# Second part of a hybrid diffusion layer: gates ahead of spatial mixing, small steps between gates, two-input work from POOL to DVE, attention output in buffers of its own

## The chip, the cores and the metric

The kernel runs on one core of one Trainium2 chip. The metric is the device time of one execution in microseconds (us), the median of three runs.

## What is computed

One layer over 2048 latent tokens of width 1024, in float32. Two token mixers read the same normalised and modulated input `h`; a sigmoid gate per channel merges them; an output projection and a layer norm close the first half, and a mixture of experts with a second layer norm the second half. The reference, cut:

```python
mod = silu(c) @ w_ada + b_ada
sh1, sc1, g1, sh2, sc2, g2 = split(mod, 6)
h = layernorm(x) * (1 + sc1) + sh1
q, k, v, u, vg, ga, gb = split_proj(h @ w_in)      # 512, 128, 128, 512, 512, 1024, 1024
y_attn = latent_attention(rope(q), rope(k), v, k_ctx, v_ctx, sink, mask)   # (2048, 512)
vn = layernorm(gelu(vg), gm_ln_g, gm_ln_b)         # in chunks of 128 tokens, 8 groups of 64
y_gm = gelu(u) * (gm_ws @ vn + gm_bs)              # spatial mixing: (128 x 128) per group
y = sigmoid(ga) * (y_attn @ w_pa) + sigmoid(gb) * (y_gm @ w_pb)
x = layernorm(ALPHA * x + g1 * (y @ w_o), ln1_g, ln1_b)
h2 = layernorm(x) * (1 + sc2) + sh2
x = layernorm(ALPHA * x + g2 * hier_moe(h2), ln2_g, ln2_b)   # router: 4 groups of 8 experts, top 1, top 2
```

## The kernel before

Every float32 product is made of three passes: an operand is split into a rounded high part (a copy on ACT) and a low part (a subtraction, usually on DVE), and high x high, low x high and high x low are added up in PSUM. `split` (L90) records both instructions, `wsplit` (L728) loads a weight piece of 128 x 1024 into one of `RAW` = 3 raw buffers and splits it into one of `WB` = 3 pairs `Wh`, `Wl`; `mm3` (L735) issues the three matmuls.

There are three parts. `pass1` does the modulation, the projections for attention and the attention itself. `pass2`, which the change is about, takes the tokens in four groups of 512. `moe` and `final` follow.

For each group g, `pass2` has these stages:

- `head(g)` (L782) multiplies `h` by the weights of u into four PSUM banks. It is also where u goes through Gelu (`gelu_u`, L806), where vg is loaded, put through Gelu, normalised (`ln_affine`, L774) and split, and where the spatial mixing (L820 to L827) stands. `MMB` = 4 banks exist for products, so the first gate can have a bank only when Gelu has emptied one.
- `gates(g, f)` (L852) makes both gates of the 128 output channels f: two products of 24 matmuls each and a sigmoid on ACT.
- `mixers(g)` (L830) transposes the spatial result on PE and splits it into `gh`, `gl`; it also loads the attention output, through the raw buffers of the weights, and splits it into `oh`, `ol`.
- `merge(f, ...)` (L864) multiplies both mixers by their weights (24 matmuls), applies the gates on DVE, adds the two halves on POOL (L872) and splits the sum into `yh`, `yl`.
- `out_proj` (L875) does the output projection for groups 0 to 2, with the low parts of its weights on POOL, and multiplies by g1. Group 3 goes through `last_tiles` (L1026) instead, whose instructions are put in order by a small planner with written durations; `wo_piece` (L928) has multiplied the weights by g1 on POOL before.

Between the steps f of a group, small work of other stages is inserted: in group 0 `rows_ada` (L747) makes the rows g1, sh2, sc2; in groups 1 to 3 the four tiles of the group before go through `norms` (L890: residual, layer norm, second norm, whose last multiply and add, L903 and L904, are on POOL), `logits` (L908) and `route_tile` (L1264, the router). `ln_stats` (L94) computes mean and variance on DVE and then, with three small POOL instructions, 1/sqrt(var + eps) and the shift.

The program is written in Python order, and the framework's scheduler decides the order on each engine: it takes ready instructions by a timing model, earlier written ones first, unless one is pinned with `keep_in_program_order`. Each engine then executes its own list strictly in that order. All loads of these stages are issued from SP's queue.

Of the kernel before, what the change touches and what calls it, by code (L numbers as in the profile page):

```python
# [18 lines left out]
P = 128  # L19
# [74 lines left out]
def ln_stats(k, pool, x, width, eps=None, pin=False):  # L94
# [606 lines left out]
def pass2(k):  # L701
    nc, tc, T = k.nc, k.tc, k.T
    k.late = k.ctx.enter_context(tc.tile_pool(name="late", bufs=1, reuse_waits="tile"))
    with ExitStack() as ctx:
# [42 lines left out]
        def rows_ada(dst, cb, one):  # L747
# [34 lines left out]
        def head(g):  # L782
# [19 lines left out]
            gm = []  # L802
            for n in ("gmg", "gmb"):
                gm.append(wk.tile([P, 512], F32, name="sg", tag="sg", bufs=2 * AHEAD + 2))
                nc.sync.dma_start(gm[-1], bcast_row(T[n], 512))
            def gelu_u(i):  # L806
                nc.scalar.activation(uy[:, 0, i, :], acc[i], AF.Gelu_apprx_tanh)  # L807

            for i in range(4):
                if i >= 2:  # L810
                    gelu_u(2 * i - 4)
                    gelu_u(2 * i - 3)
                vg = wk.tile([P, 512], F32, name="vg", tag="vg", bufs=2)
                nc.sync.dma_start(vg, k.vg_d[4 * g + i])
                nc.scalar.activation(vg, vg, AF.Gelu_apprx_tanh)
                ln_affine(vg, 512, gm[0], gm[1], vg)
                split(k, vv[:, 0, i, :], vv[:, 1, i, :], vg)
# [12 lines left out]
        def mixers(g):  # L830

            uy = st[g][1]
            gT, oT = [], []
            for j in range(4):
                tp = tr_bank()
                for i in range(4):
# [976 lines left out]
```

## Time and profile before

| | us |
|---|---|
| median of 3 runs (2435.75 to 2441.88) | 2441.51 |
| the profiled execution, its own time | 2448.21 |
| its span, first to last instruction | 2446.4 |
| busy PE | 2232.2 |
| busy DVE | 1749.7 |
| busy ACT | 1200.7 |
| busy POOL | 913.7 |

The profiled execution is 6.7 us above the median. PE is TensorE's matmuls, DVE is VectorE, ACT is ScalarE, POOL is GpSimd, SP is the engine whose queue issues the loads. Busy time is an average over stages with different limits. `pass2` lasts from about 556 us (the last attention matmul) to about 1500 us; the out projections of groups 0 to 2 end at about 794, 1024 and 1255 us.

### The profile page before, as it was taken

What the parts mean: (1) busy time and instruction counts of PE and PEld (TensorE: products, weight loads), DVE (VectorE), ACT (ScalarE), POOL (GpSimd) and SP (SyncE); (2) the same over time, 40 slices, a digit from 0 to 9 for tenths busy, and PEclk for the clock granted to TensorE, in tenths of its full rate; (3) what the DMA queues carried; (4) which work ended last, traced back from release to release, by engine and by line L of the source; (5) the groups of instructions that cost most, each with busy time, mean ns of one, the idle gap of its engine ahead of it and who ended that gap; (6) DMA issues with size and microseconds to landing.
All of it is one profiled execution on the core that took longest, in us unless ns stands there. A gap on an engine that the chain in (4) does not pass through costs nothing. (4 is left out here: it accounts for less than half of the span.)

```text
span 2446.4 us, 32062 instructions
## 1 busy us (share of the span) xinstructions
PE 2232.2 (91%) x11269; PEld 1827.5 (75%) x11269; DVE 1749.7 (72%) x2925; ACT 1200.7 (49%) x1655; POOL 913.7 (37%) x767
## 2 busy tenths in 40 slices
PE   7899999998999899989999998799999998999960
PEld 3799999986768787877877776577777786777750
DVE  3778888886763677468547877478897868758868
ACT  3566666665222433343333323266575756546645
POOL 2333333421003432344324354233452536225328
PEclk9999999999999999999999998799999999999995
DMA  8211111116564445444344434589998989868956
GB/s 300 67 53 57 57 56 40 48 40 225 184 213 136 158 138 160 151 147 146 104 138 155 137 88 189 185 281 319 327 340 271 330 253 326 267 196 321 344 161 250
DMA packets 126711, 449.88 MB, mean 184 GB/s; under 512 B 20762, under 2 KB 42194, under 8 KB 101972
## 3 DMA queue, kind: packets, MB, share of 16 engines
q1 hardware_dynamic: 113684, 405.82, 47.5%
q0 software_dynamic: 12864, 41.98, 7.6%
q8 instruction: 90, 1.47, 0.2%
q14 instruction: 73, 0.60, 0.1%
HBM read 383.18 MB, written 64.57 MB: 183 GB/s over the span
## 5 line engine op out<-in xcount | busy, mean ns | idle before, releaser
L91 DVE TENSOR_TENSOR mWl<-mraw,mWh 128x2048 fp32r<-128x2048 f32 x192 | 437.5, 2311 | 57.5 <-ACT mWh L91 56.6
L91 ACT CAST mWh<-mraw 128x2048 fp32r<-128x2048 f32 x192 | 359.0, 1906 | 104.3 <-PE h L1551 79.3
L1551 PE MATMUL h<-mWh,xh 128*128 128x512 f32 x784 | 219.3, 400 | 5.7 <-ACT xh L91 4.5
L738 PE MATMUL mm<-hh,Wl 128*128 128x512 f32 x512 | 207.1, 404 | 10.7 <-DVE Wl L91 10.5
L737 PE MATMUL mm<-hh,Wh 128*128 128x512 f32 x512 | 207.2, 405 | 8.9 <-ACT yh L807 8.3
L1598 POOL DMA_INDIRECT acc_d<-yo,lst x49 | 140.7, 2871 | 199.0 <-DVE yo L1592 131.4
L91 ACT CAST Wh<-raw 128x1024 fp32r<-128x1024 f32 x140 | 145.8, 1046 | 138.8 <-PE mm L739 56.0
L1551 PE MATMUL h<-mWl,xh 128*128 128x512 f32 x784 | 212.8, 393 | 0.0
L739 PE MATMUL mm<-hl,Wh 128*128 128x512 f32 x512 | 206.2, 403 | 0.0
L91 DVE TENSOR_TENSOR Wl<-raw,Wh 128x1024 fp32r<-128x1024 f32 x116 | 157.5, 1362 | 53.4 <-ACT Wh L91 53.2
L1551 PEld LDWEIGHTS h<-mWh,xh 128*128 128x128 f32 x784 | 145.3, 190 | 37.3 <-ACT xh L91 5.4
L1551 PEld LDWEIGHTS h<-mWl,xh 128*128 128x128 f32 x784 | 148.8, 190 | 32.0
L1597 POOL TENSOR_TENSOR yo<-yo,g2b 64x1024 f32<-64x1024 f32 x20 | 119.9, 5997 | 125.7 <-DVE yo L1595 117.9
L379 PE MATMUL pj<-wh,hTl 128*128 128x512 f32 (+1 forms) x400 | 147.5, 369 | 3.3 <-POOL hTl L361 2.6
L379 PE MATMUL pj<-wh,hTh 128*128 128x512 f32 (+1 forms) x400 | 148.5, 372 | 1.5 <-DVE hTh L360 1.4
L379 PE MATMUL pj<-wl,hTh 128*128 128x512 f32 (+1 forms) x400 | 148.2, 371 | 0.0
L1516 POOL DMA_INDIRECT xg<-h_d,lst x49 | 73.5, 1500 | 169.2 <-PE tr L1530 90.2
L1551 PE MATMUL h<-mWh,xl 128*128 128x512 f32 x464 | 127.6, 396 | 8.6 <-DVE xl L91 8.4
L872 POOL TENSOR_TENSOR sg<-sg 128x512 f32<-128x512 f32 x32 | 44.4, 1388 | 239.1 <-DVE sg L871 215.8
L537 DVE CUSTOM_DVE_ANT_0 Sb<-S,mask,sink 128x640 f32<-128x640 f32 (+1 forms) x128 | 110.2, 861 | 23.4 <-PE S L533 16.6
L738 PEld LDWEIGHTS mm<-hh,Wl 128*128 128x128 f32 x512 | 99.7, 195 | 35.7 <-DVE Wl L91 15.3
L1551 PE MATMUL y<-mWh,gh 128*128 128x512 f32 x392 | 112.6, 407 | 13.0 <-DVE gh L91 11.7
(387 smaller groups left out, 5688.3 us busy)
## 6 DMA issues: line engine op xcount, KB each, us to landing
mraw<-mw SPq DMA_DIRECT2D x192, 1024.0 KB
raw<-wf SPq DMA_DIRECT2D x96, 512.0 KB
raw<-ada SPq DMA_DIRECT2D x32, 512.0 KB
raw<-wo SPq DMA_DIRECT2D x32, 512.0 KB
x<-x SPq DMA_DIRECT2D x30, 512.0 KB
x<-ada SPq DMA_DIRECT2D x16, 512.0 KB
hT_d<-hf SPq DMA_DIRECT2D x32, 256.0 KB
raw<-hT_d SPq DMA_DIRECT2D x16, 512.0 KB
```

What stands on the lines that cost most here:

```text
L91: return k.nc.scalar.copy(hi, src), (eng or k.nc.vector).tensor_sub(lo, src, hi)
L379: ins = nc.tensor.matmul(box[0][:, :n], x[:, kc, ts], y[:, kc, c0:c0 + n], start=q == 0, stop=q == 3 * KC - 1)
L537: nc.vector.tensor_tensor_reduce(x[:, :nk], S[:, :nk], mask[:, mi, :nk], 1.0, sink[:, h:h + 1], OP.add, OP.max, mx[:, s:s + 1])
L737: nc.tensor.matmul(out, lh, rh, start=first, stop=False)
L738: nc.tensor.matmul(out, ll, rh, start=False, stop=False)
L739: nc.tensor.matmul(out, lh, rl, start=False, stop=last)
L872: nc.gpsimd.tensor_add(sg[0], sg[0], sg[1])
L1516: ins = nc.gpsimd.indirect_dma_start(out=xg[i][0:n, :], out_offset=None, in_=k.h2_d[:, :], in_offset=bass.IndirectOffsetOnAxis(ap=lists[s] ...
L1551: nc.tensor.matmul(accs[m], a[:, ks], b[:, c0:c0 + 512], start=first and i + j == 0, stop=last and j == 1 and i == len(t) - 1)
L1597: nc.gpsimd.tensor_tensor(yo[0:64], yo[0:64], g2[0:64], op=OP.mult)
L1598: nc.gpsimd.indirect_dma_start(out=k.acc_d[:, :], out_offset=bass.IndirectOffsetOnAxis(ap=l[0:n, j, 0:1], axis=0), in_=yo[0:n, :], in_offs ...
```

## The change

All of it is in `ln_stats` and in `pass2`.

- Order: `head` only issues the products. `gelu_u`, `norm_v` (one tile of vg), `spatial`, `gate` (one gate), `mixers` (spatial result only) and `attended` (attention output only) are functions of their own. The new order is: head, Gelu of u, vg tiles 0 and 1, both gates of f = 0, vg tiles 2 and 3, spatial mixing, then per f: first gate of f + 1, (at f = 0 the mixers), the small steps `between`, second gate of f + 1, merge of f, the steps `behind`.
- Small steps: in `between` the transposes and splits of the router's input (`logit_rows`) and the norms; in `behind` the router's matmuls, the first part of `route_tile` for tile t - 1 and its rest for tile t - 2. `rows_ada` moves to `between`, and its two matmuls are put off by one step (`finish`).
- From POOL to DVE: the sum in `merge`, the low parts of the weights in `out_proj`, the last multiply and add of the second norm (which now takes `ln_affine` in place of an ACT instruction and two on POOL), the multiplication by g1 (now in `residual`, on the result), the addition of eps and the shift in `ln_stats`; of the latter only the power stays on POOL.
- Buffers: the attention output is loaded into the two buffers `x` of the norms, no longer into the raw weight buffers; `rows_ada` uses `th`, `tl` and no longer `Wh`, `Wl`; the second half of `logit_rows` uses the two buffers of `vg`.
- `out_proj` sorts the last weight piece by tile, and multiplies by g1 as soon as one accumulator is finished.

```diff
 def ln_stats(...)
-    nc.vector.tensor_scalar(mv[:, 5:6], mv[:, 0:1], -1.0, None, op0=OP.mult)
-    nc.gpsimd.tensor_add(mv[:, 2:3], mv[:, 1:2], k.epst if eps is None else eps)
+    nc.vector.tensor_scalar(mv[:, 2:3], mv[:, 1:2], LN_EPS if eps is None else eps, None, op0=OP.add)
     nc.gpsimd.tensor_tensor(mv[:, 3:4], mv[:, 2:3], k.mhalf, op=OP.pow)
-    nc.gpsimd.tensor_tensor(mv[:, 4:5], mv[:, 5:6], mv[:, 3:4], op=OP.mult)
+    if shift:
+        nc.vector.scalar_tensor_tensor(mv[:, 4:5], mv[:, 0:1], -1.0, mv[:, 3:4], op0=OP.mult, op1=OP.mult)
...
+        def gelu_u(g):
             for i in range(4):
-                if i >= 2:
-                    gelu_u(2 * i - 4)
-                    gelu_u(2 * i - 3)
...
+                nc.scalar.activation(st[g][1][:, 0, i, :], st["acc"][i], AF.Gelu_apprx_tanh)
+        def norm_v(g, i):
...
+        def spatial(g):
...
+        def attended(g):
+            oT = []
             for jp in range(2):
-                raw = piece(k.oT_d[g, :, 2 * jp:2 * jp + 2, :].rearrange("p a b -> p (a b)"))
+                raw = wk.tile([P, D], F32, name="x", tag="x", bufs=2)
+                nc.sync.dma_start(raw, k.oT_d[g, :, 2 * jp:2 * jp + 2, :].rearrange("p a b -> p (a b)"))
...
+        def gate(g, f, m):
...
-            nc.gpsimd.tensor_add(sg[0], sg[0], sg[1])
+            nc.vector.tensor_add(sg[0], sg[0], sg[1])
...
-                W = {h: wsplit(T["wo"][h, :, 2 * kp:2 * kp + 2, :].rearrange("p a b -> p (a b)"), nc.gpsimd) for h in hs}
+                W = {h: wsplit(T["wo"][h, :, 2 * kp:2 * kp + 2, :].rearrange("p a b -> p (a b)")) for h in hs}
+                steps = [(j, u) for j in range(2) for u in units]
+                if kp == 3:
+                    steps.sort(key=lambda x: units.index(x[1]))
...
-            if quick:
-                ln_affine(r, D, sc2, sh2, h2, k.epsa)
-            else:
-                mu, rs, nmr = ln_stats(k, wk, r, D, k.epsa)
-                nc.scalar.activation(h2, r, AF.Identity, bias=nmr, scale=rs)
-                nc.gpsimd.tensor_tensor(h2, h2, sc2, op=OP.mult)
-                nc.gpsimd.tensor_tensor(h2, h2, sh2, op=OP.add)
+            ln_affine(r, D, sc2, sh2, h2, LN_EPS * ALPHA * ALPHA)
...
+        def logit_rows(h2):
...
+                hi, lo = (wk.tile([P, 512], F32R, name=n, tag="vg" if q else n, bufs=2 if q else 1) for n in ("th", "tl"))
...
         def wo_piece(h, kp):
-            nc.gpsimd.tensor_tensor(r3, r3, g1[:, None, h * 512:(h + 1) * 512].to_broadcast([P, 2, 512]), op=OP.mult)
...
                 def residual(h):
+                    nc.vector.tensor_tensor(box[h], box[h], g1[:, sl], op=OP.mult)
                     nc.vector.scalar_tensor_tensor(x[:, sl], x[:, sl], ALPHA, box[h], op0=OP.mult, op1=OP.add)
...
+        def between(g, f):
+            while due:
+                due.pop(0)()
+            if g == 0:
+                if f < 6:
+                    due.append(rows_ada(g1 if f < 2 else sh2 if f < 4 else sc2, f, 1.0 if f // 2 == 2 else 0.0))
+                return
+            t = 4 * (g - 1) + f
+            if 1 <= f < 5:
+                turned[t - 1] = logit_rows(h2s[t - 1])
+            if f < 4:
+                with tc.issue_after(st["mixed"]):
+                    h2s[t] = norms(t, rr[f])
+            if g == 1 and f in (5, 6):
+                due.append(rows_ada(None, f + 1, 0.0))
+        def behind(g, f):
+            t = 4 * (g - 1) + f
+            if g and 2 <= f < 6:
+                for _ in routes[t - 2]:
+                    pass
+            if g and 1 <= f < 5:
+                routes[t - 1] = route_tile(k, wk, ps, logits(turned[t - 1]), t - 1)
+                for _ in range(3):
+                    next(routes[t - 1])
         for g in range(4):
             head(g)
-            sgs = [gates(g, f) for f in range(AHEAD)]
-            X2 = mixers(g)
+            gelu_u(g)
+            norm_v(g, 0)
+            norm_v(g, 1)
+            sgs = [[gate(g, 0, m) for m in range(2)]]
+            norm_v(g, 2)
+            norm_v(g, 3)
+            spatial(g)
             for f in range(8):
-                if f + AHEAD < 8:
-                    sgs.append(gates(g, f + AHEAD))
+                sg = []
+                if f + 1 < 8:
+                    sg.append(gate(g, f + 1, 0))
+                if f == 0:
+                    gT = mixers(g)
+                    X2 = (attended(g), gT)
+                between(g, f)
+                if f + 1 < 8:
+                    sg.append(gate(g, f + 1, 1))
+                    sgs.append(sg)
                 merge(f, sgs[f], X2, yh, yl)
+                behind(g, f)
```

## Rows read from the trace of the kernel before

**Rows 1.** The page's first part: busy time of each engine in us, share of the span, instructions.

```profile
PE 2232.2 (91%) x11269; PEld 1827.5 (75%) x11269; DVE 1749.7 (72%) x2925; ACT 1200.7 (49%) x1655; POOL 913.7 (37%) x767
```

**Rows 2.** [...] The first four are groups 0 to 3, cut at the end of each out projection; the fifth is the first 60 us after group 3's last merges began.

```profile
556.00:794.00 238.00, 215.75 (x925) 171.61 (x925) 138.05 (x185) 82.35 (x102) 40.73 (x34) 0.98 0.60 193
794.00:1024.00 230.00, 218.98 (x1009) 180.12 (x1008) 158.66 (x302) 79.81 (x111) 85.62 (x68) 0.98 0.49 152
1024.00:1255.00 231.00, 218.48 (x1008) 180.27 (x1008) 141.47 (x284) 78.75 (x109) 83.45 (x68) 0.98 0.43 132
1255.00:1437.00 182.00, 170.27 (x793) 140.19 (x793) 129.98 (x260) 64.45 (x94) 68.20 (x55) 0.97 0.45 137
1437.00:1497.00 60.00, 54.63 (x232) 44.39 (x232) 46.07 (x65) 16.11 (x20) 38.75 (x34) 0.94 0.27 93
```

**Rows 3.** Whom PE waited for from 556 to 1560 us: waiting line, releaser, us in total, times, longest in us.

```profile
PE mm L738 <- DVE Wl L91: 11.1, 10, 2.0
PE mm L737 <- ACT Wh L91: 11.0, 7, 6.1
PE mm L737 <- ACT gh L91: 10.6, 4, 3.1
PE lg L1314 <- DVE M L1294: 9.9, 4, 3.2
PE mm L737 <- ACT yh L807: 8.3, 4, 3.0
...
PE mm L737 <- DVE rr L888: 3.8, 3, 1.6
...
PE mm L1047 <- DVE wol L91: 2.7, 1, 2.7
```

**Rows 4.** Five windows of 10 us in which the granted clock fell; columns as in Rows 2.

```profile
846.00:856.00 10.00, 6.88 (x30) 5.38 (x29) 5.71 (x7) 3.37 (x5) 8.41 (x6) 0.86 0.64 211
...
1076.00:1086.00 10.00, 6.91 (x29) 5.49 (x28) 5.92 (x7) 3.61 (x5) 8.41 (x6) 0.83 0.61 210
...
1156.00:1166.00 10.00, 10.00 (x41) 8.09 (x40) 3.01 (x7) 1.72 (x3) 2.56 (x2) 0.78 0.36 127
...
1386.00:1396.00 10.00, 9.88 (x38) 8.33 (x38) 3.67 (x15) 2.12 (x3) 2.03 (x2) 0.67 0.32 101
...
1436.00:1446.00 10.00, 6.82 (x24) 5.42 (x24) 6.54 (x11) 3.26 (x4) 6.92 (x4) 0.83 0.55 184
```

**Rows 5.** Timeline at the start of group 2's first gate: start, length, engine, line, operation; in brackets the idle time before and its releaser.

```profile
1047.51 1.04 ACT L91 CAST oh<-raw 128x1024 fp32r<-128x1024 f32 x1 [2.12 <-DMA raw<-oT_d]
...
1049.62 0.50 PE L737 MATMUL mm<-hh,Wh 128*128 128x512 f32 x1 [3.01 <-ACT yh L807]
```

**Rows 6.** Timeline of group 2's first merge, of three engines.

```profile
1074.54 3.28 POOL L904 TENSOR_TENSOR x<-x,sh 128x1024 f32<-128x1024 f32 x1
...
1078.39 1.03 PE L837 MATMUL tr<-ident,yh 128*128 128x128 f32 x8
...
1080.75 1.24 ACT L902 ACTIVATE x<-rr,mv 128x1024 f32<-128x1024 f32 x1 [3.33 <-POOL mv L108]
...
1082.51 0.79 PE L737 MATMUL mm<-gh,Wh 128*128 128x512 f32 x1 [3.09 <-ACT gh L91]
```

**Rows 7.** Timeline of one tile's routing in group 1, of three engines.

```profile
914.10 2.40 POOL L903 TENSOR_TENSOR x<-x,sc 128x1024 f32<-128x1024 f32 x1 [1.21 <-ACT x L902]
...
914.48 2.04 DVE L1279 TENSOR_SCALAR dl<-l,gm 128x4 f32<-128x4 f32 x1
...
923.15 0.18 PE L1314 MATMUL lg<-M,tri 128*128 128x32 bf16 x1 [3.14 <-DVE M L1294]
```

**Rows 8.** Timeline of group 3's last merges, POOL and DVE.

```profile
1439.65 3.15 POOL L932 TENSOR_TENSOR raw<-raw,g 128x1024 f32<-128x1024 f32 x1 [0.20 <-DMA raw<-wo]
...
1440.58 3.31 DVE L91 TENSOR_TENSOR wol<-raw,woh 128x1024 fp32r<-128x1024 f32 x1
```

**Rows 9.** Groups of DVE instructions by line and form, 556 to 1500 us, and the ACT table loads ahead of Gelu in the same stretch: line, engine, operation, out<-in, form, count, busy us, mean ns, idle before.

```profile
L91 DVE TENSOR_TENSOR Wl<-raw,Wh 128x1024 fp32r<-128x1024 f32 x116 | 157.5, 1362 | 53.4 <-ACT Wh L91 53.2
L871 DVE TENSOR_TENSOR sg<-sg,mm 128x512 f32<-128x512 f32 x64 | 43.4, 682 | 35.8 <-PE mm L739 35.5
...
L91 DVE TENSOR_TENSOR yl<-sg,yh 128x512 fp32r<-128x512 f32 x32 | 31.9, 998 | 2.0 <-ACT yh L91 2.0
L100 DVE BATCH_NORM_STATS2 st<-rr 128x6 f32<-128x512 f32 x48 | 30.5, 681 | 0.2
...
L777 DVE SCALAR_TENSOR_TENSOR rr<-rr,mv,ln1g 128x1024 f32<-128x1024 f32 x12 | 15.3, 1279 | 0.0
...
L1279 DVE TENSOR_SCALAR dl<-l,gm 128x4 f32<-128x4 f32 x12 | 11.2, 936 | 0.0
...
L815 ACT ACT_TABLE_LOAD x5 | 6.4, 1283 | 21.1 <-DMA vg<-vg_d 21.1
```

**Rows 10.** Three of these DVE operations by tile: count, shortest/median/longest in ns, first and last start.

```profile
L91 DVE TENSOR_TENSOR Wl<-raw,Wh x116: 1200/1222/2919, 562.5 to 1439.3; 128x1024 fp32r<-128x1024 f32 x116
...
L91 DVE TENSOR_TENSOR yl<-sg,yh x32: 672/684/4582, 641.0 to 1460.4; 128x512 fp32r<-128x512 f32 x32
...
L1279 DVE TENSOR_SCALAR dl<-l,gm x11: 209/213/2054, 892.8 to 1398.6; 128x4 f32<-128x4 f32 x11
```

More of the change, by code (lines that the diff above doesn't have):

```diff
@@ L801, in head @@
                         [x[:, j * 512:(j + 1) * 512] for x in W], kc == 0, kc == KC - 1)
[L802 to L807, printed above, removed]
-            for i in range(4):
-                if i >= 2:
-                    gelu_u(2 * i - 4)
-                    gelu_u(2 * i - 3)
[L813 to L817, printed above, removed]
+            st[g] = (hT, uy)
+            st["vv"], st["gm"], st["acc"] = vv, [], acc
+        def gelu_u(g):
+            for i in range(4):
+                nc.scalar.activation(st[g][1][:, 0, i, :], st["acc"][i], AF.Gelu_apprx_tanh)
+        def norm_v(g, i):
+            gm, vv = st["gm"], st["vv"]
+            if not gm:
+                for n in ("gmg", "gmb"):
+                    gm.append(wk.tile([P, 512], F32, name="sg", tag="sg", bufs=2 * AHEAD + 2))
+                    nc.sync.dma_start(gm[-1], bcast_row(T[n], 512))
+            vg = wk.tile([P, 512], F32, name="vg", tag="vg", bufs=2)
+            nc.sync.dma_start(vg, k.vg_d[4 * g + i])
+            nc.scalar.activation(vg, vg, AF.Gelu_apprx_tanh)
+            ln_affine(vg, 512, gm[0], gm[1], vg)
+            split(k, vv[:, 0, i, :], vv[:, 1, i, :], vg)
+        def spatial(g):
+            uy, vv = st[g][1], st["vv"]
             if g == 0:
@@ L914, in logits @@
                     nc.tensor.transpose(tp[:, j * P:(j + 1) * P], h2[:, kc * P:(kc + 1) * P], k.ident)
-                hi = wk.tile([P, 512], F32R, name="th", tag="th", bufs=1)
-                lo = wk.tile([P, 512], F32R, name="tl", tag="tl", bufs=1)
+                hi, lo = (wk.tile([P, 512], F32R, name=n, tag="vg" if q else n, bufs=2 if q else 1) for n in ("th", "tl"))
                 split(k, hi, lo, tp)
-                for j in range(4):
-                    kc = 4 * q + j
-                    for a, y in enumerate((hi, lo)):
-                        nc.tensor.matmul(lg, y[:, j * P:(j + 1) * P], rws[:, kc, :],
-                                         start=kc == 0 and a == 0, stop=kc == KC - 1 and a == 1)
+                parts.append((hi, lo))
+            return parts
+        def logits(parts):
+            lg = ps.tile([P, 72], F32, name="lg", tag="lg", bufs=2)
+            for kc in range(KC):
+                for a, y in enumerate(parts[kc // 4]):
+                    nc.tensor.matmul(lg, y[:, kc % 4 * P:(kc % 4 + 1) * P], rws[:, kc, :],
+                                     start=kc == 0 and a == 0, stop=kc == KC - 1 and a == 1)
             l = wk.tile([P, 36], F32, name="l", tag="l")
@@ L1075, in norm @@
                     d = add("Pool", 0.95, root, d)
+                    d = add("DVE", 0.15, shift, d)
                     out = []
@@ L1118, in steps @@
                         last[0] = plan.add("PE", 0.86, lambda h=h, q=q: out_chunk(h, q), [last[0]])
-                    d.append(add("DVE", 0.67, lambda h=h: residual(h), last[0]))
+                    d.append(add("DVE", 1.35, lambda h=h: residual(h), last[0]))
                 ends.append(last[0])
-                d = norm(x, lambda: x, ln1g, ln1b, k.epst, d)
+                d = norm(x, lambda: x, ln1g, ln1b, LN_EPS, d)
                 add("SP", 0.1, lambda: nc.sync.dma_start(k.acc_d[(t + 1) * P:(t + 2) * P, :], x), *d)
@@ L1180, in pass2 @@
                         split(k, rws[:, :, 0:36], rws[:, :, 36:72], rwr)
[L1181 to L1196 removed]
+                if g == 3 and f == 6:
+                    first_expert(k, wk, ps)
                 if g == 3 and f > 5:
```

105 lines of the change are left out of this document (44 added, 61 removed).

## The prediction, made before the changed kernel was run

> **What bounds the kernel now.** I read the page's busy shares first. PE is busy for 91% of the span and no other engine is near it [rows 1], so an edit pays only where it removes a wait of PE or a stretch at a low clock, and PE's own work is not changed. Next the windows by stage [rows 2]: in the second part the four groups last 238, 230, 231 and 182 us, with PE busy for 215.75, 218.98, 218.48 and 170.27 us. PE is thus idle for 22.3 + 11.0 + 12.5 + 11.7 = 57.5 us. The mean clock is 0.98, 0.98, 0.98 and 0.97. [...] The 60 us after that lose 5.4 us to idling and 0.06 x 60 = 3.6 us to the clock. All that the change can win is therefore 57.5 + 19.5 + 9.0 = 86 us, less some 8 us of the entry into the second part, whose 6.1 us wait (the longest in the second row of [rows 3]) and the slow start behind it are not touched: 78 us, 3.2% of the time.
>
> The list of PE's waits says for whom [rows 3]. Apart from the entry they are low parts of weights on DVE (11.1 us), the split of the transposed mixer result `gh` (10.6), the router's one-hot `M` (9.9), Gelu of u, which frees a PSUM bank (8.3), `Wh` (11.0 - 6.1 = 4.9), the residual multiply `rr` (3.8) and `wol` (2.7). After a wait of some 3 us the granted clock falls: the windows around or behind them show 0.86, 0.83, 0.78, 0.67, 0.83, which is up to 10 x (1 - clock), so 1.4 to 3.3 us each [rows 4].
>
> The timelines show that three of these waits begin elsewhere. At group 2's first gate ACT's list had the cast `oh` of the attention output in front of Gelu of u; its load landed late, ACT idled 2.12 us, and PE then waited 3.01 us for the bank [rows 5]. At the first merge the transposes stand at 1078.39, but the casts of `gh` are queued on ACT behind the norm's L902, which waited 3.33 us for POOL, which was busy with L904 until 1077.8; PE waited 3.09 us [rows 6]. In the routing, L1279 on DVE, a scalar operation on 128x4, took 2.04 us and ended within 0.1 us of POOL's L903 (914.48 + 2.04 = 916.52; 914.10 + 2.40 = 916.50); PE waited 3.14 us for `M` behind it [rows 7]. At the end of group 3, the low part `wol` took 3.31 us beside POOL's multiply by g1 [rows 8]. So POOL's long two-input work costs twice: it is slow, and DVE stands still beside it.
>
> **The change, part by part.** Prices are in PE time.
>
> *Gelu ahead, attention output in own buffers.* Gelu of u is now written right behind the head, and the load and cast of the attention output come after a gate, through buffers that are free since the last norm of the group before. The wait for the bank (8.3 us, 4 times [rows 3]) has as cover the 18 matmuls that follow the last one of the head's first bank (the head's last weight piece is sorted by bank). I take 6 us of it; bounds 0, if ACT's list still has another operation with a late load in front, and 8.3.
>
> *Mixers apart from the merge.* Between the spatial mixing and the first merge there now stand two single gates of 24 matmuls, where the casts can run. L902 and the two POOL steps behind which they stood are gone. 10.6 us [rows 3] and 1.4 + 1.7 us of clock in two of the windows [rows 4] are there; I take 11 of 13.7, with bounds 5 and 13.7.
>
> *Router.* Its first part is emitted a step ahead of its matmul, and L903 and L904 no longer hold DVE. 9.9 us of waits [rows 3] and 2.2 + 3.3 us of clock behind two of them [rows 4], 15.4 us: I take 13, bounds 6 and 15.4.
>
> *Weights of the last tiles.* Without POOL's multiply the split no longer queues behind it and the raw buffers come free earlier. `wol` 2.7 us, some 3 us of `Wh` [rows 3], 1.7 us of clock [rows 4], in a stage that idles 5.4 us and loses 3.6 to the clock [rows 2]: I take 7, bounds 3 and 9.
>
> *Low parts of weights and the out projection.* 11.1 us of `Wl` and 3.8 us of `rr` [rows 3]. `rows_ada` gives up the weights' buffers and has its matmuls a step later; the last weight piece is sorted by tile, so that the multiply by g1 no longer comes in a bunch. I take 9 of 14.9, bounds 3 and 14.9.
>
> Gains together: 6 + 11 + 13 + 7 + 9 = 46 us, between 17 and 51.
>
> *What DVE takes over.* 32 sums at 0.684, the median of `yl`, which also reads two SBUF operands of 128x512 [rows 10]: 21.9 us. 24 low parts in the out projections at 1.222 [rows 10]: 29.3. 12 tiles x 2 long operations at 1.279, as L777 [rows 9]: 30.7. 8 multiplies by g1 at 0.682, as L871 [rows 9]: 5.5. Sum 87.4 us. What it gets back is the stretching beside POOL, mean less median: (1.362 - 1.222) x 116 = 16.2 for `Wl`, (0.998 - 0.684) x 32 = 10.0 for `yl`, (0.936 - 0.213) x 12 = 8.7 for L1279 [rows 9, 10], 34.9 us in three groups alone. Net 52.5 us more on DVE. Its busy time over the four groups is 138.05 + 158.66 + 141.47 + 129.98 = 568 of 881 us [rows 2]; it would rise to 621 us, 70%. DVE does not become the bound on the average.
>
> It may in the steps with a norm. Such a step has 72 matmuls; at 218.98 us for 1009 instructions [rows 2] they take 15.6 us. DVE has in it three low parts (3.7), two gate products, a sum and `yl` (2.7), a norm of five operations at 1.279 and four statistics at 0.681 [rows 9] (9.1), two low parts of `logit_rows` (1.4): 16.9 us, and the router's small operations, which I estimate at 3 us: 20. That is 4 us too many in each of 12 steps, 48 us if PE pays all of it; 0 if the norm, whose result is wanted only a step later, gives way to the weights, which have three buffers of cover, and is made up in the steps without one. I take 8 us, nearer to nothing, since before the change the same steps ran with 14 us plus the stretching and PE's waits there were the router's, not `Wl`.
>
> *Small things.* The residual of the last tile has one more DVE operation of 0.682 on the chain that leads to the experts, and two fewer POOL operations in each of its norms: 0 to +0.7 us, I take 0.3. In the first part and in the second the shift moves to DVE, where it waits for POOL's power in line and holds what is behind it; 18 tiles at 0 to 0.3 us, 0 to 5 us, and the shorter chain on POOL may give the same back: -5 to +5, I take 0. The loads are the same; only the attention output's eight leave the weights' raw buffers. The experts' part does not change and only begins earlier.
>
> Sum: -46 + 8 + 0.3 = -37.7 us.
>
> **The rivals.** *Almost all waits go* (-65 us): the gains at their upper bounds (51), and clock windows that I have not counted (19.5 + 3.6 us in all, of which the terms hold 10.3), with nothing paid for DVE. For it: the waits hang on few causes. Against it: a new order has waits of its own. 2441.5 - 65 = 2376.
>
> *The tables.* Tiles 2 and 3 of vg are now written behind the sigmoids of the first gates. If ACT's list follows that order, Gelu and sigmoid alternate once more in each group: 8 more table loads at 1.283 us [rows 9], 10.3 us on ACT, on the path only where one stands ahead of a cast or of a bank's release. ACT's share in the four groups is 35% [rows 2]. If all are paid: 38 - 10 = 28, 2414; with a quarter of the gains (11 us) missing as well, 2425. [...]
>
> *No change.* The lists come from a timing model, and program order is only a preference; the same waits could come back at other places, the gain being that of POOL alone: the last weights' 7 us less the 8 us of DVE, 2442.
>
> *DVE becomes the bound* (slower): the 12 steps with a norm each cost PE more than 4.5 us, 54 us in all, against 46 us of gain. At 5 us each the sum is -46 + 60 = +14 us: 2456. For it: the 20 us against 15.6. Against it: the weights' buffers and the lighter steps 5 to 7 of each group. It decides from about 3.8 us a step (46 / 12).
>
> **How the numbers follow.** The median is 6.7 us below the profiled execution (2448.2), so the span should come to about 2446.4 - 38 = 2408 us, and the time to 2448.2 - 38 = 2410 for a like execution, 2404 against the median. Chances: my sum 0.60 (2385 to 2424), almost all waits go 0.15, tables and a partial gain 0.12, no change 0.07, DVE the bound 0.06. Range 2370 to 2434, which leaves out the slower case and half of no change. A difference below 0.3% (7 us) can't be told from none. Faster 0.87, same 0.07, slower 0.06.
>
> **What would show it.** In the profile after: no wait for `yh` at the first gates and at most one of the `gh` waits; no `M` among PE's waits; L1279 at its median of 0.2 us everywhere; `Wl` on DVE with mean near 1.23; POOL's busy time in the second part below a third of before; groups 1 and 2 in some 218 us instead of 230. Wrong would be: waits of PE for `Wl` above 25 us in groups 1 to 3, which is DVE as the bound; more than 12 table loads in the second part with PE waiting behind them; or the first part's end moved from 556 us by more than 5 us.

## The result, and the profile after

The changed kernel takes 2386.8 us (median of 4 runs, 2381.7 to 2389.1) against 2440.5 (4 runs, 2435.8 to 2441.9): 53.7 us less, ratio 0.9782 with a 95% interval of 0.9766 to 0.9798. It lies inside the predicted range and 17 us below the predicted 2404, at the lower edge of the 2385 to 2424 that the sum was given. The profiled execution of after took 2381.7 us with a span of 2379.9, its shortest, while that of before was its longest (2448.2), so the two traces differ by 66 us and some 13 us of that are no gain of the change. The stretch from the first expert matmul to the end, whose code is the same, is 6 us shorter in the trace of after (883.5 against 889.4).

The page's first part of the kernel after, to be held beside [rows 1]: busy us, share of the span, instructions.

```profile
PE 2203.3 (93%) x11269; PEld 1810.2 (76%) x11269; DVE 1748.7 (73%) x3039; ACT 1193.6 (50%) x1649; POOL 688.6 (29%) x547
```

POOL has lost 225 us of work, DVE has 114 instructions more, and DVE's busy time is the same to 1 us. The prediction had 52 us more there.

The four groups of the second part after, as windows like those of [rows 2]: start and end, length, then busy time and instructions of PE, PEld, DVE, ACT and POOL, TensorE's granted clock (1.00 is full speed), DMA share, GB/s. The last window runs to group 3's last output-projection matmul:

```profile
558.00:782.00 224.00, 211.57 (x919) 172.56 (x919) 147.04 (x202) 83.94 (x104) 4.65 (x6) 0.96 0.64 208
782.00:1002.00 220.00, 214.81 (x1012) 177.46 (x1011) 157.21 (x328) 80.26 (x111) 26.69 (x20) 1.00 0.52 160
1002.00:1220.00 218.00, 214.22 (x1010) 177.26 (x1011) 146.15 (x308) 76.28 (x107) 23.96 (x20) 1.00 0.45 141
1220.00:1396.00 176.00, 172.77 (x829) 142.83 (x828) 126.50 (x291) 64.18 (x94) 22.90 (x18) 1.00 0.48 148
1396.00:1438.00 42.00, 42.00 (x191) 34.70 (x190) 29.63 (x53) 10.56 (x15) 15.29 (x14) 1.00 0.18 64
```

PE's idle time in the groups is 12.4 + 5.2 + 3.8 + 3.2 = 24.6 us where it was 57.5, and from group 1 on the granted clock is 1.00; group 0 is at 0.96. Whom PE waits for, from 540 to 1520 us, as in [rows 3]:

```profile
PE mm L737 <- ACT Wh L91: 6.9, 3, 6.1
PE mm L738 <- DVE Wl L91: 6.1, 5, 2.0
PE tr L846 <- DVE yh L836: 5.6, 4, 4.2
...
PE lg L1360 <- DVE M L1340: 1.4, 2, 1.0
PE mm L737 <- DVE rr L902: 1.4, 3, 0.7
...
PE mm L737 <- ACT gh L91: 0.7, 3, 0.2
PE mm L737 <- ACT yh L810: 0.6, 3, 0.2
```

`gh` fell from 10.6 to 0.7 us, `M` from 9.9 to 1.4, `yh` at the first gates from 8.3 to 0.6, `Wl` from 11.1 to 6.1. The wait at the entry (6.1) stays, and the one ahead of group 0's transposes has grown from 1.1 to 4.2 us. On DVE, by tile (shortest/median/longest in ns), beside [rows 10]:

```profile
L91 DVE TENSOR_TENSOR Wl<-raw,Wh x140: 1169/1220/1227, 564.2 to 1387.9; 128x1024 fp32r<-128x1024 f32 x140
...
L91 DVE TENSOR_TENSOR yl<-sg,yh x32: 666/683/694, 645.9 to 1400.6; 128x512 fp32r<-128x512 f32 x32
...
L1325 DVE TENSOR_SCALAR dl<-l,gm x16: 209/210/213, 867.6 to 1468.4; 128x4 f32<-128x4 f32 x16
```

The longest cases of 2.9, 4.6 and 2.1 us are gone; each of the three operations now stays within 60 ns of its median.

### The profile page after: what moved, and what is told of

It is laid out like the page before. It is cut to its first block, busy times and chain, and to the rows that moved or that the text cites. A ratio compares the mean times of both kernels' runs of the same rounds, so it can differ in the third digit from the quotient of the medians.

```text
span 2379.9 us, 31840 instructions
## 1 busy us (share of the span) xinstructions
PE 2203.3 (93%) x11269; PEld 1810.2 (76%) x11269; DVE 1748.7 (73%) x3039; ACT 1193.6 (50%) x1649; POOL 688.6 (29%) x547
## 5 line engine op out<-in xcount | busy, mean ns | idle before, releaser
L106 POOL TENSOR_TENSOR mv<-mv,mhalf 128x1 f32<-128x1 f32 x58 | 58.6, 1013 | 663.3 <-DVE mv L105 657.0
L91 DVE TENSOR_TENSOR Wl<-raw,Wh 128x1024 fp32r<-128x1024 f32 x140 | 170.3, 1219 | 75.7 <-ACT Wh L91 75.0
L738 PE MATMUL mm<-hh,Wl 128*128 128x512 f32 x512 | 200.5, 392 | 6.1 <-DVE Wl L91 6.1
L737 PE MATMUL mm<-hh,Wh 128*128 128x512 f32 x512 | 202.3, 395 | 1.3 <-ACT yh L810 0.6
L739 PE MATMUL mm<-hl,Wh 128*128 128x512 f32 x512 | 200.2, 391 | 0.0
L91 ACT CAST ph<-pt 128x512 fp32r<-128x512 f32 x184 | 93.4, 521 | 73.4 <-PE pt L568 69.9
L544 ACT ACTIVATE Sb<-Sb,mx 128x641 f32<-128x641 f32 (+1 forms) x128 | 105.4, 824 | 41.3 <-DVE mx L539 31.9
L537 DVE CUSTOM_DVE_ANT_0 Sb<-S,mask,sink 128x640 f32<-128x640 f32 (+1 forms) x128 | 110.1, 860 | 19.5 <-PE S L533 17.5
```

The source lines that it names most:

```text
L91: return k.nc.scalar.copy(hi, src), (eng or k.nc.vector).tensor_sub(lo, src, hi)
L537: nc.vector.tensor_tensor_reduce(x[:, :nk], S[:, :nk], mask[:, mi, :nk], 1.0, sink[:, h:h + 1], OP.add, OP.max, mx[:, s:s + 1])
L544: nc.scalar.activation(Sb[s][:, :nk + 1], Sb[s][:, :nk + 1], AF.Exp, bias=mx[:, 2 + s:3 + s], scale=1.0, accum_out=mx[:, 4 + s:5 + s])
L737: nc.tensor.matmul(out, lh, rh, start=first, stop=False)
L738: nc.tensor.matmul(out, ll, rh, start=False, stop=False)
L739: nc.tensor.matmul(out, lh, rl, start=False, stop=last)
```

## The experiments

Three questions: which half of the change pays, the order or the moves; why POOL's work cost so much; and how much of DVE is left. All runs are timed in 3 rounds, the last in 5, beside runs of the kernel before (medians 2439.5, 2438.6, 2440.2 and 2437.2 us in the four series). The first table gives the time, the second the stages: from the first matmul of one group's head to that of the next, in us, read from the timelines of one execution each (group 3 to its last output-projection matmul).

| run | median us | ratio to before, 95% interval |
|---|---|---|
| the change | 2386.8 | 0.9782 (0.9766 to 0.9798) |
| e1, moves alone | 2403.2 | 0.9856 (0.9836 to 0.9876) |
| e2, order alone | 2407.7 | 0.9870 (0.9850 to 0.9891) |
| e3, attention output in raw | 2393.3 | 0.9810 (0.9792 to 0.9828) |
| e4, experts' multiply on DVE | 2393.5 | 0.9811 (0.9790 to 0.9832) |
| e5, moves and sorted piece | 2397.1 | 0.9824 (0.9808 to 0.9840) |
| e6, idle work on POOL | 2426.9 | 0.9946 (0.9929 to 0.9962) |
| e7, fills on POOL | 2390.8 | 0.9797 (0.9781 to 0.9814) |
| e8, idle work on DVE | 2385.3 | 0.9777 (0.9761 to 0.9794) |
| e9, three times the fills | 2392.2 | 0.9843 (0.9774 to 0.9912) |
| e10, e5 and rows_ada | 2389.8 | 0.9796 (0.9764 to 0.9829) |
| e11, mixers a gate later | 2386.4 | 0.9789 (0.9760 to 0.9819) |
| e12, last normalisation on DVE | 2382.4 | 0.9768 (0.9751 to 0.9785) |

| stage | before | after | e1 | e2 | e5 | e6 | e8 | e9 | e10 |
|---|---|---|---|---|---|---|---|---|---|
| group 0 | 230.1 | 217.4 | 229.4 | 220.4 | 227.8 | 229.4 | 217.9 | 218.9 | 220.7 |
| group 1 | 231.2 | 220.4 | 223.7 | 225.9 | 220.5 | 231.0 | 218.7 | 219.6 | 220.3 |
| group 2 | 231.2 | 217.6 | 221.9 | 217.1 | 219.7 | 236.3 | 218.3 | 220.5 | 219.9 |
| group 3 | 240.3 | 218.1 | 215.8 | 231.3 | 219.2 | 217.8 | 216.9 | 217.6 | 218.3 |

A stage is known to about 2 us: e11, whose instruction lists turned out to be those of the change, has 219.3, 220.1 and 218.2 in groups 0 to 2.

**e1: the moves alone.** Before's order and buffers, with every place where the change makes POOL's work DVE's; the core of it:

```diff
-            nc.gpsimd.tensor_add(sg[0], sg[0], sg[1])
+            nc.vector.tensor_add(sg[0], sg[0], sg[1])
...
-                W = {h: wsplit(T["wo"][h, :, 2 * kp:2 * kp + 2, :].rearrange("p a b -> p (a b)"), nc.gpsimd) for h in hs}
+                W = {h: wsplit(T["wo"][h, :, 2 * kp:2 * kp + 2, :].rearrange("p a b -> p (a b)")) for h in hs}
...
-                nc.scalar.activation(h2, r, AF.Identity, bias=nmr, scale=rs)
-                nc.gpsimd.tensor_tensor(h2, h2, sc2, op=OP.mult)
-                nc.gpsimd.tensor_tensor(h2, h2, sh2, op=OP.add)
+            ln_affine(r, D, sc2, sh2, h2, LN_EPS * ALPHA * ALPHA)
...
-            nc.gpsimd.tensor_tensor(r3, r3, g1[:, None, h * 512:(h + 1) * 512].to_broadcast([P, 2, 512]), op=OP.mult)
```

> The order and the buffers of the kernel before, with all of the work moved from POOL to DVE. Theory of the prediction (the order is what pays; POOL's work only stretched some DVE operations): the last weights' 7 us and part of the router's 13 us come, DVE's 8 us are paid, so 2425 to 2440 us, with PE's waits for gh and yh as before (10 and 8 us). Rival (POOL's work beside DVE was most of the 54 us): at or below 2405 us, with the waits for gh and M gone although the order is the old one.

Measured: 2403.2 us, 36.3 less than before. The theory of the prediction falls and the rival holds. Its waits of PE, 540 to 1520 us:

```profile
PE mm L737 <- ACT yl L91: 20.5, 3, 6.9
...
PE mm L738 <- DVE Wl L91: 4.8, 5, 2.4
...
PE mm L737 <- ACT gh L91: 0.7, 3, 0.2
...
PE lg L1310 <- DVE M L1290: 0.4, 1, 0.4
PE mm L737 <- ACT yh L807: 0.2, 1, 0.2
```

`gh` and `M` are gone in the old order. A new wait of 20.5 us in three places has come, at the next group's head. The timeline at the end of group 1, of two engines:

```profile
1016.33 1.23 DVE L91 TENSOR_TENSOR hl<-raw,hh 128x1024 fp32r<-128x1024 f32 x1 [4.04 <-ACT hh L91]
...
1017.48 2.47 DVE L888 TENSOR_TENSOR rr<-mm,g 128x512 f32<-128x512 f32 x4
...
1018.31 0.77 PE L737 MATMUL mm<-Wh,hh 128*128 128x512 f32 x1 [6.76 <-ACT yl L91]
```

The multiplies that free the PSUM banks stand in DVE's list behind `hl` of the next group, whose load was late (the cast `hh` ahead of it waited 4.40 us for it). DVE idles 4 us ahead of work that could have been done; of the four multiplies in 2.47 us the first ends, by an even division, near 1018.1, and PE starts 0.2 us behind it. The name `yl` in the row is only the last of several semaphores.

**e2: the order alone.** The changed kernel with all of e1's places given back to POOL.

> The changed kernel with the moved work put back on POOL; order and own buffers stay. Theory of the prediction: the order alone gives 30 to 40 of the 54 us, so 2395 to 2410 us; Wl on DVE goes back to a mean near 1.36 us. Rival (the moves are most of it): 2420 us or more, with PE waiting for M and for Wl.

Measured: 2407.7 us, 31.8 less than before; here the theory of the prediction holds. So each half alone gives some 60 to 70% of the gain, and 36.3 + 31.8 = 68.1 is 14 more than both together give: they remove in part the same waits. The order removes `gh` and most of `M` without touching POOL; with POOL's work left, `Wl` keeps its long cases (waits of PE and the tile's row; its mean is 1.38 us):

```profile
PE mm L738 <- DVE Wl L91: 11.0, 6, 2.8
...
PE mm L1062 <- DVE wol L91: 4.2, 1, 4.2
...
PE lg L1361 <- DVE M L1341: 2.8, 1, 2.8
...
PE mm L737 <- ACT gh L91: 1.0, 4, 0.2
```

```profile
L91 DVE TENSOR_TENSOR Wl<-raw,Wh x116: 1204/1218/3001, 562.1 to 1399.8; 128x1024 fp32r<-128x1024 f32 x116
```

The stages say where each half works: group 0 is the order's (230.1 to 220.4 in e2, 229.4 in e1), group 3 mostly the moves' (215.8 in e1, 231.3 in e2), and in groups 1 and 2 either does most of it.

**e5 and e10: which of the order's edits is left to do once POOL is out of the way.** e5 adds to e1 the sorted last weight piece with the multiply behind each tile; e10 adds to e5 `rows_ada` on the `th` and `tl` buffers, its matmuls a step later.

```diff
                 steps = [(j, u) for j in range(2) for u in units]
+                if kp == 3:
+                    steps.sort(key=lambda x: units.index(x[1]))
...
+                    if kc == KC - 1:
+                        sl = slice(h * 512, (h + 1) * 512)
+                        nc.vector.tensor_tensor(rr[i][:, sl], acc[i, h], g1[:, sl], op=OP.mult)
```

> The kernel before, the work moved from POOL to DVE, and one edit of the order: the last weight piece of each out projection sorted by tile, with the multiply by g1 right behind each tile. In the run of the moves alone PE waited 20.5 us in three places at the next group's head, where the bank to be written still had its multiply by g1 to come. Theory (POOL's two-input work was in the causes of the other waits, and this bunch was the one that the moves left): those three waits go, 2380 to 2390 us, the time of the whole change, so that the rest of the order adds nothing to it. Rival (the new order of gates and mixers is still worth something without POOL's work): 2392 to 2403 us.

Measured: 2397.1 us. The wait of 20.5 us is gone from the list, yet the rival's range holds. The stages show where the rest lies: groups 1 to 3 are those of the changed kernel to 2 us, and group 0 is 10 us behind.

```diff
-            ah = wr.tile([P, 512], F32R, name="ah", tag="Wh", bufs=WB)
-            al = wr.tile([P, 512], F32R, name="al", tag="Wl", bufs=WB)
+            ah = wk.tile([P, 512], F32R, name="ah", tag="th", bufs=1)
+            al = wk.tile([P, 512], F32R, name="al", tag="tl", bufs=1)
...
-                        rows_ada(g1 if f < 2 else sh2 if f < 4 else sc2, f, 1.0 if f // 2 == 2 else 0.0)
+                        due.append(rows_ada(g1 if f < 2 else sh2 if f < 4 else sc2, f, 1.0 if f // 2 == 2 else 0.0))
```

> The kernel before with the moves, the sorted last weight piece, and as its only other edit rows_ada on buffers of its own with its two matmuls a step later. The run without this last edit was 2397.1 us, and stage by stage it was behind the changed kernel in group 0 alone (227.8 us from head to head against 217.4; 220.5 and 219.7 in groups 1 and 2 against 220.4 and 217.6). If that is rows_ada's doing: 2385 to 2390 us, the whole gain without gates ahead, spatial mixing behind them, or small steps. If it is the order of gates and mixers in group 0: 2394 to 2400 us.

Measured: 2389.8 us, group 0 at 220.7. Moves, sorted piece and `rows_ada` together can't be told from the whole change (intervals 0.9764 to 0.9829 and 0.9766 to 0.9798). What is left for early Gelu, own buffers, gates ahead of the mixing and small steps is 3 us at this resolution. e10's trace still has the wait that the early Gelu removes, and why it costs no more than that is not shown:

```profile
PE mm L737 <- ACT yh L810: 7.7, 4, 2.6
```

**e6, e7 and e9: why POOL's work cost so much.** To the changed kernel, work that nobody reads is added at the places from which POOL's was taken, into a buffer that is otherwise idle there. e6 multiplies two SBUF operands; e7 fills the same tile with zeros; e9 is e7 with three fills for each, so that POOL is busy for as long as in e6.

```diff
+        def extra(n): return [(lambda z: nc.gpsimd.tensor_tensor(z, g1[:, 0:512], g1[:, 512:1024], op=OP.mult))(wk.tile([P, 512], F32, name='aacc', tag='aacc', bufs=1)) for _ in range(n if g1 is not None else 0)]
...
+                W = {...}; extra(2)
...
+            ln_affine(r, D, sc2, sh2, h2, LN_EPS * ALPHA * ALPHA); extra(4)
...
+                merge(f, sgs[f], X2, yh, yl); extra(1 if g and not (g == 1 and f in (5, 6)) else 0)
```

> The changed kernel with 118 two-input multiplies of 128x512 on POOL that nobody reads, at the places from which POOL's work was taken (4 in each norm, 1 in each merge of groups 1 to 3, 2 at each weight pair of the out projections of groups 0 to 2), some 160 us of POOL. Theory (POOL's work holds up DVE's while it runs): DVE's Wl rises from a mean of 1.22 to 1.3 us and more with longest cases of 2 to 3 us, and the time by 10 us or more. Rival (POOL's work was late only for those who wait for its results): DVE's times and the time as in the changed kernel, within 5 us, apart from the power of the norm, which stands behind these multiplies in POOL's list.

> As the run with the two-input multiplies, but each of the 118 is a fill of the same tile with zeros, which reads nothing from SBUF; every other engine has the same list of instructions as there. If what holds DVE up is POOL's reading of SBUF: Wl stays at 1.22 us and the time within 5 us of the changed kernel. If any work on POOL does it, or the norm's power standing behind it in POOL's list: as slow as with the multiplies, in proportion to POOL's time.

> The run with the fills, three fills in the place of each one: 354 of 0.53 us, 188 us of POOL, nearly the 205 us that the 118 two-input multiplies took. If the multiplies cost their 40 us because POOL was busy, or because the norm's power stood behind them in POOL's list: 2410 to 2427 us. If they cost them because they read SBUF while DVE reads two operands there: 2385 to 2397 us, with DVE's Wl never above 1.25 us.

Measured: 2426.9, 2390.8 and 2392.2 us. The multiplies cost 40 us, three quarters of what the change gained, though nothing reads them; fills that hold POOL almost as long cost about 5, which the intervals can't tell from nothing. (One of e9's four runs took 2420.8 us, the other three 2389.6 to 2392.6; hence its ratio and its wide interval.) The norm's power stands behind the fills in POOL's list as it does behind the multiplies, so e9 rules out that this place in the list is the price. By stages, the 16 multiplies of group 0, all in its out projection, cost 12 us, and the 24 of group 3, in norms and merges, none; why these were free is not shown, as DVE is busy for 73% and 72% of the two stages. The POOL group of e6, then that of e9, 558 to 1470 us:

```profile
L886 POOL TENSOR_TENSOR aacc<-g 128x512 f32<-128x512 f32 x118 | 205.2, 1739 | 119.3 <-DVE al L91 110.6
```

```profile
L886 POOL MEMSET aacc<- 128x512 f32 x354 | 186.7, 527 | 128.6 <-DVE al L91 108.9
```

DVE's operations in e6 over the second part, by group (mean in ns behind the comma):

```profile
L91 DVE TENSOR_TENSOR Wl<-raw,Wh 128x1024 fp32r<-128x1024 f32 x140 | 197.3, 1414 | 59.8 <-ACT Wh L91 59.3
L883 DVE TENSOR_TENSOR sg<-sg,mm 128x512 f32<-128x512 f32 x64 | 43.4, 679 | 20.5 <-PE mm L739 20.4
...
L100 DVE BATCH_NORM_STATS2 st<-rr 128x6 f32<-128x512 f32 x48 | 30.5, 682 | 0.1
...
L781 DVE SCALAR_TENSOR_TENSOR vg<-vg,mv,sg 128x512 f32<-128x512 f32 x16 | 17.9, 1135 | 0.8 <-POOL mv L106 0.5 <-DMA sg<-gmb 0.3
```

`Wl`, with both operands in SBUF, went from 1219 to 1414 ns on the mean and L781 from 745 to 1135; `sg*mm`, the product with the gate, one of whose operands is in PSUM (679 in the changed kernel and in e6), and the statistics, which read one tensor (681 and 682), did not move. In e6 12 of the 64 `sg*mm` and 7 of these 48 statistics began while one of the multiplies ran, and none took more than 0.70 us; of the 140 `Wl` 32 did, and 29 of them took 1.29 to 2.34 us. One place in e6 shows how the multiplies cost time:

```profile
1073.78 1.28 POOL L886 TENSOR_TENSOR aacc<-g 128x512 f32<-128x512 f32 x1
1073.84 2.30 DVE L781 SCALAR_TENSOR_TENSOR x<-x,mv,sh 128x1024 f32<-128x1024 f32 x1 [0.44 <-POOL mv L106]
...
1076.58 2.28 DVE L781 SCALAR_TENSOR_TENSOR rr<-rr,mv,ln1b 128x1024 f32<-128x1024 f32 x1 [0.44 <-POOL mv L106]
1078.78 2.28 DVE L91 TENSOR_TENSOR Wl<-raw,Wh 128x1024 fp32r<-128x1024 f32 x1
...
1081.11 0.80 PE L738 MATMUL mm<-hh,Wl 128*128 128x512 f32 x1 [9.98 <-DVE Wl L91]
```

POOL starts 0.06 us ahead of DVE and is done at 1075.06; DVE, whose operation takes 1.28 us in the changed kernel, ends at 1076.14, 1.08 us behind POOL: as if it had waited for POOL's to end and run then. Three such stand ahead of the matmul, and PE stood for 10 us. In e9 `Wl` is never above 1.23 us:

```profile
L91 DVE TENSOR_TENSOR Wl<-raw,Wh x140: 1170/1220/1228, 567.1 to 1393.6; 128x1024 fp32r<-128x1024 f32 x140
```

Beside POOL's multiplies, then, `Wl` was held (29 of 32), and `sg*mm` and the statistics were not (none above 0.70 us); beside its fills `Wl` was not held either (none of 140 above 1.23 us). By what means one engine holds the other no run shows.

Not every operation that reads one tensor was free. In the trace of before small copies, casts and scalar operations were held as well: L1279 is one [rows 7], 2.04 us for 0.21, the cast at L1289 another, 1.18 us for 0.17, and this copy of 128x4, 0.17 us at the median, ended 0.02 us behind POOL's add. Why these were held and the statistics were not, no run here shows.

```profile
1354.70 2.40 POOL L904 TENSOR_TENSOR x<-x,sh 128x1024 f32<-128x1024 f32 x1
1354.70 2.42 DVE L1271 COPY g<-l 128x4 f32<-128x4 f32 x1
```

**e8: how much of DVE is left.** The 118 multiplies of e6 on DVE.

```diff
-nc.gpsimd.tensor_tensor(z, g1[:, 0:512], g1[:, 512:1024], op=OP.mult)
+nc.vector.tensor_tensor(z, g1[:, 0:512], g1[:, 512:1024], op=OP.mult)
```

> The changed kernel with the same 118 multiplies on DVE, about 0.68 us each, 80 us more on DVE. If DVE has the slack that the prediction gave it on the average (577 of 881 us busy in the second part): within 8 us of the changed kernel. If DVE is at its limit in the steps with a norm, as the prediction feared: 20 to 60 us more, with PE waiting for Wl in groups 1 to 3.

Measured: 2385.3 us, no slower than the changed kernel, with DVE busy for 72 us more:

```profile
PE 2209.8 (93%) x11269; PEld 1818.1 (76%) x11269; DVE 1820.9 (76%) x3157; ACT 1194.3 (50%) x1649; POOL 690.8 (29%) x547
```

Nor does PE wait longer for `Wl` than after (6.1 us):

```profile
PE mm L738 <- DVE Wl L91: 5.6, 5, 1.7
```

The same 118 multiplies thus cost 40 us on POOL and nothing on DVE.

**e3: the attention output through the raw buffers.**

```diff
-                raw = wk.tile([P, D], F32, name="x", tag="x", bufs=2)
-                nc.sync.dma_start(raw, k.oT_d[g, :, 2 * jp:2 * jp + 2, :].rearrange("p a b -> p (a b)"))
+                raw = piece(k.oT_d[g, :, 2 * jp:2 * jp + 2, :].rearrange("p a b -> p (a b)"))
```

> The changed kernel with the attention output loaded through the weights' raw buffers again, nothing else. If the own buffers carry part of the 6 us put down to the early Gelu: 2390 to 2395 us, with PE waiting for the cast oh or for Wh near the first merge. If the gate written ahead hides that load anyway: 2384 to 2390 us, within what the runs can tell from the changed kernel.

Measured: 2393.3 us, where the first theory put it; its interval and that of the changed kernel overlap. In the trace PE's waits for `Wh` are 12.5 us where they were 6.9, and for `rr` 5.3 where they were 1.4. That the own buffers pay is likely, but not settled.

**e4 and e12: the lesson tried at two other places.** POOL still has 20 multiplies in the experts and 10 operations in the last normalisation.

```diff
-                nc.gpsimd.tensor_tensor(yo[0:64], yo[0:64], g2[0:64], op=OP.mult)
+                nc.vector.tensor_tensor(yo[0:64], yo[0:64], g2[0:64], op=OP.mult)
```

> The changed kernel with one more move: the 20 multiplies of 64x1024 by g2 in the experts go from POOL (117.6 us for 19 in its trace) to DVE. If POOL's two-input work stretches DVE's in that part too and PE pays for it: 5 to 15 us less than the changed kernel. If PE's waits there (28 us in all) are the order's own: within 3 us of it, and DVE's mean for the experts' low parts stays near 2.31 us. If DVE becomes late: up to 10 us more.

Measured: 2393.5 us, 7 above the changed kernel (intervals just overlap). POOL's row in the changed kernel shows why nothing was to be had:

```profile
L1643 POOL TENSOR_TENSOR yo<-yo,g2b x20: 2373/3388/11580, 1586.5 to 2297.0; 64x1024 f32<-64x1024 f32 x20
```

Here it is POOL that is held, up to 11.6 us for an operation of 2.4, beside DVE's long `mWl` (2.28 us, one behind another), and the trace shows no wait of PE for it. One of the longest cases begins 0.16 us behind DVE:

```profile
1635.16 2.27 DVE L91 TENSOR_TENSOR mWl<-mraw,mWh 128x2048 fp32r<-128x2048 f32 x1
...
1635.32 11.58 POOL L1643 TENSOR_TENSOR yo<-yo,g2b 64x1024 f32<-64x1024 f32 x1 [9.13 <-DVE yo L1641]
```

On DVE the multiply takes 1.21 us; from the first expert matmul to the end DVE's busy time rises from 672.9 to 688.8 us, and PE's waits for `xl` from 5.5 to 10.1.

```diff
-FPG = (0, 2, 4, 6, 8, 12, 13)
-FPB = (3, 7, 13)
+FPG = ()
+FPB = ()
```

> The changed kernel with the 10 multiplies and adds of 128x1024 that POOL still has in the last normalisation put on DVE; nothing else. In the changed kernel's trace DVE does the other 22 there in 37.9 us (1.17 us the shortest, 3.4 the longest) and POOL its 10 in 27.4. Theory (POOL's two-input work is done in DVE's time): 32 operations at 1.17 to 1.21 us are 37.4 to 38.7 us, so DVE has no more busy time than now for 10 operations more, POOL's small steps of the statistics get shorter, and the time is 0 to 6 us less. Rival (there the two engines do share the work): DVE 12 us busier in the last 65 us and 5 to 12 us more time.

Measured: 2382.4 us, 4.4 below the changed kernel; the intervals overlap, so a gain isn't shown. The groups are as expected, after and then e12:

```profile
L1783 DVE TENSOR_TENSOR r<-r,gb 128x1024 f32<-128x1024 f32 x13 | 20.7, 1620 | 3.8 <-POOL r L1782 3.8
...
L1782 DVE TENSOR_TENSOR r<-r,gb 128x1024 f32<-128x1024 f32 x9 | 17.2, 1906 | 3.0 <-ACT r L1781 3.0
```

```profile
L1782 DVE TENSOR_TENSOR r<-r,gb 128x1024 f32<-128x1024 f32 x16 | 19.2, 1213 | 1.3 <-ACT r L1781 1.3
L1783 DVE TENSOR_TENSOR r<-r,gb 128x1024 f32<-128x1024 f32 x16 | 19.1, 1219 | 0.0
```

32 operations in 38.3 us instead of 22 in 37.9: POOL's ten had cost DVE as much time as doing them itself.

**e11: the mixers' transposes a gate later.**

```diff
-                    gT = mixers(g)
-                    X2 = (attended(g), gT)
+                    oT = attended(g)
...
+                if f == 0:
+                    X2 = (oT, mixers(g))
```

> The changed kernel with the transposes of the spatial mixing behind the second gate of step 0 instead of the first, directly ahead of the merge, whose first 12 matmuls are those of the attention output. In the changed kernel PE waits 5.6 us for yh ahead of the transposes, 4.2 us of it in group 0 with the clock at 0.66 around it. If that wait goes and the 12 matmuls cover the casts of gh: 3 to 6 us less than the changed kernel, 2381 to 2384 us. If PE waits for gh instead: 5 to 12 us more.

Measured: 2386.4 us, with the 4.2 us wait for `yh` where it was. It tests nothing: the instruction lists that came out of both texts are the same on every engine. As a repetition it says how far a time can be trusted: 0.4 us between the two medians.

## Why the prediction was right, and where it was off

**The bound and the ceiling** held. PE was the bound, the gain came out of its waits and its slow stretches, and 53.7 of the 78 us were won. The ceiling's 19.5 us of slow stretches are what the four clocks of [rows 2] lack to 1.00, times the lengths: 4.8 + 4.6 + 4.6 + 5.5. At the lowest, as from 1082 to 1084 us of before, the granted clock was 0.50, and a 128x512 matmul started every 0.43 us there, against every 0.23 us at 1.00. The reading that the clock falls after a wait of some 3 us has an exception in its own rows: behind the wait of 3.01 us at 1049.62 [rows 5] the granted clock stayed at 1.00 until 1082.

**One sum is wrong.** The upper bounds of the five gains, 8.3 + 13.7 + 15.4 + 9 + 14.9, add up to 61.3 us and not to 51. With 61.3 the rival "almost all waits go" would be at about -74 us, 2367, and the measured 2386.8 lies between it and the sum; against the 2376 as written it lies nearer to the rival.

**Each named wait went, and for the cause named, but the credit was not divided.** The prediction wrote 11 us to "Mixers apart from the merge" and 13 to the router, for waits that it had traced to POOL (L902 waiting behind L904, L1279 standing beside L903); both terms name the new place and the end of POOL's steps together. e1 keeps the old order and has 0.7 us of `gh` and 0.4 of `M`; e2 keeps POOL's work and has 1.0 and 2.8. The stall needed both a DVE or ACT operation held by POOL and a matmul close behind it; to take away either is nearly enough. Hence the two halves overlap by 14 us.

**The DVE term was mis-sized**, and this is 8 of the 17 us. The prediction moved 87.4 us on to DVE, gave 34.9 back "in three groups alone", and charged 8 us (0 to 48) for the norm's steps. Measured: all of it came back (1749.7 us busy before, 1748.7 after), and a further 72 us cost nothing (e8). Summed over all its operations, what DVE took above the median of each was 105 us before and is 33. The three groups were not all that had been stretched: L778 on `vg` was 1195 ns and is 745 (7.2 us in 16), L1292 506 and 233 (6.6 us in 24), L1268 694 and 190 (6.0 us in 12). The sentence "DVE stands still beside it" was right, but was priced by three rows, when the trace of before shows it at L778, L1292 and L1268 as well, and at small copies and casts (2.42 and 1.18 us for 0.17).

The other 9 us are not settled. By the prediction's own measure the two traces give 57.5 - 24.6 = 32.9 us of idling and 19.5 - 9.0 = 10.5 of clock in the groups, and 9.0 behind them, 52 us against the 46 of its gains; but these traces differ by 13 us more than the medians do. That the time fell into the range of the sum was in part luck: it is 2 us above that range's lower end.

**The rival "no change"** priced "the gain being that of POOL alone" at 7 us less the 8 of DVE. e1 gives 36.3. **"DVE becomes the bound"** needed 3.8 us in each norm step; e8 shows none even with four multiplies more in each.

**The other terms.** *Last weights*, 7: from the first output-projection matmul of group 3 to its last, 55.5 us before, 49.3 after and in e1, 56.3 in e2, so 6.2, and the moves'. *`Wl` and out projection*, 9: the two waits fell from 14.9 to 7.5; e5 and e10 show 6 and 7 us for its two edits, in medians whose neighbouring intervals overlap. *Gelu*, 6: the wait fell by 7.7, and what the time shows is 3 (e10 against the change) to 6.5 (e3), neither outside the noise. *First part*: its end moved by 1.7 us (556.4 to 558.1), inside the 5 allowed.

**The tables.** The rival's condition came true for the most part, without its price. There are 16 table loads in the second part instead of 10, where it had 8 more; these are the two large groups:

```profile
L821 ACT ACT_TABLE_LOAD x8 | 10.3, 1283 | 29.8 <-DMA vg<-vg_d 29.7
L873 ACT ACT_TABLE_LOAD x7 | 9.0, 1283 | 0.1
```

PE's wait for the bank that Gelu frees is 0.6 us, and ACT had 64% of its time free there. Where the next operation was ready, a switch held ACT for 1.31 us, from 595.91 to 597.22 here:

```profile
595.28 0.63 ACT L821 ACTIVATE vg<-vg 128x512 f32<-128x512 f32 x1 [0.60 <-DMA vg<-vg_d]
595.93 1.28 ACT L873 ACT_TABLE_LOAD   x1
597.22 0.60 ACT L873 ACTIVATE sg<-mm 128x512 f32<-128x512 f32 x1
```

**The signs.** `Wl` at a mean of 1.22, L1279 at 0.21 throughout, POOL in the four groups at 78 us of 278 (28%), groups 1 and 2 in 220.4 and 217.6 us: as announced. "No `yh`", "no `M`" and "at most one `gh`" fail by the letter (0.6 us in 3, 1.4 in 2, 0.7 in 3) and hold in substance. None of the three signs of being wrong came: PE's waits for `Wl` are 6.1 us and not 25, PE hardly waits behind the table loads, and the first part's end stayed. Not announced was the 4.2 us wait for `yh` in group 0.

## What to carry over

Where two engines stretch each other's instructions, price a move by the time that both get back: compare the longest and the median duration of each operation on the receiving engine first, all of them and not the three worst. In the second part of this kernel operations moved from POOL to DVE were nearly free (DVE was busy for 1749.7 us before and 1748.7 after) and paid (36.3 us in e1), as DVE was the one that was held and PE waited behind it; in the experts it is POOL that is held (up to 11.6 us for 2.4), and the move gained nothing (e4, 2393.5 us against 2386.8). When two edits remove the same wait, run each alone before crediting either.

## What the hardware showed that was not expected

- Two-input operations on POOL were not free though nobody read their results: 118 of 128x512 cost 40 us (e6), 354 fills of the same buffer about 5, within the noise (e9), the same multiplies on DVE nothing (e8).
- DVE's products with one operand in PSUM (679 ns in the change and in e6) and its statistics (681 and 682) ran on beside POOL's multiplies, none that met one above 0.70 us; operations with two operands in SBUF took up to 2.3 us for 1.2 (e6). Small copies, casts and scalar operations on one tensor were held too: 2.42 us for 0.17 (L1271), 1.18 for 0.17 (L1289) and 2.05 for 0.21 (L1279, all of before).
- Either engine was held by the other: in e6 DVE, which began 0.06 us behind POOL; in the experts POOL, which began 0.16 us behind DVE and took 11.6 us for 2.4.
